# Two transformer blocks on one Trainium2 core: group ends in four steps, filters in the second layer, a reordered beginning

## The chip, the core and the metric

The kernel runs on one core of a Trainium2 chip. PE (TensorE) does the matmuls, PEld is the loading of their stationary operands, DVE (VectorE), ACT (ScalarE) and POOL (GpSimd) do the elementwise work, and SP (SyncE) issues most of the DMAs. The metric is the time of one execution in microseconds (us) on the device; less is better.

## The reference, cut to what matters

The input is x (512 tokens x 1024). Two blocks follow one another, each of two layers. A layer of the first block:

```python
def hybrid_layer(x, ...):
    h = rmsnorm(x, g_pre) @ w_in
    (a_q, a_k, a_v, b_b, b_c, b_x, c_q, c_kv, c_kr, d_q, d_k, d_v, gate) = jnp.split(h, SPLIT_IDX, axis=-1)
    ya = swa_sink_attention(a_q, a_k, a_v, sinks)      # window of 128, 4 heads
    yb = short_gated_conv(b_b, b_c, b_x, conv_w, conv_b)
    yc = mla(c_q, c_kv, c_kr, pos, g_cq, w_uq, g_ckv, w_ukv)
    yd = stick_breaking_attention(d_q, d_k, d_v)
    y = jnp.stack([ya, yb, yc, yd], axis=2)            # four groups of 256 columns
    y = rmsnorm(y, g_grp).reshape(b, s, D_MIX)         # each group by itself
    y = y * jax.nn.silu(gate)
    return x + rmsnorm(y @ w_out, g_post)
```

The second block has, in each layer, a modulation computed from two vectors (`silu(c) @ w_mod`, 1024 x 6144 a layer), attention over tokens and a context, a Fourier mix, a long convolution (Hyena) and a convolutional FFN. The filter of the long convolution depends on weights alone:

```python
def hyena_filter(L, w1, b1, fr1, w2, b2, fr2, w3):
    h = jnp.sin(fr1 * (z @ w1 + b1))                   # z: a fixed embedding of the L positions
    h = jnp.sin(fr2 * (h @ w2 + b2))
    h = h @ w3                                         # 512 columns: forward and backward filter
    two = concatenate([h[:, :256] * decay, 0, (h[:, 256:] * decay)[:0:-1]])
    return two / sum(abs(two), axis=0)
```

Three such filters are needed: for x and the context in the second block's first layer, and for x in its last. So the modulation and the filters need nothing of the first block, and can be computed beside it.

## The kernel before, in words

**Tiles.** Activations lie transposed in SBUF, features on partitions. A large matmul has float32 accuracy through three products of split operands (`mm3`, L560 to L562: high x high, high x low, low x high; L560 to L562 are therefore most of the matmul rows). Every weight tile (128 x 1024 elements, 512 KB) is loaded by SP into one of two `raw` slots and split: ACT copies it to the high part (L528), DVE subtracts for the low part (L529). The same `split` with a factor is L531 and L532.

**The beginning.** `Hybrid.begin` loads the layer's small arrays. SP then loads x in four tiles of 128 tokens (L470, L718). `norm(p)` normalizes two tiles: ACT squares and sums (L576), POOL makes mean and root (L569, L570), DVE scales (L586), PE transposes (L594), ACT and DVE split (L531, L532). `go(p)` multiplies by two kinds of weights that are kept for p = 1: `b_wc` (four tiles, 416 columns a matmul) and `b_wv`. `modulation` begins with a Tanh on ACT (L1306) of an array `cc` that is loaded by ACT's queue, and a DVE operation on it (L1308).

**The weave.** Then `weave` interleaves generators. A generator yields after each step a number, its cost; the generator with the smallest share of its given total goes on next. In a layer of the first block four run together: the attentions (`attention`: MLA's input, stick-breaking, MLA, sliding window), the projections (`dense`: 21 weight tiles `b_wa`, the gates, and last the convolution `conv`), the modulation (`mod_layer`: SP loads `w_mod` into a ring `ws` of four slots, L1336; DVE multiplies and adds, L1340 and L1342), and in layer 0 also `prep`: the sine nets (`filter_nets`, L1192 to L1200), three times `filters` (product L1217, decay L1218, absolute values on ACT L1219, sums L1221 and L1223, a matmul of ones L1227, a reciprocal L1228, output L1234 and L1235) and `fourier_weights` (L1293, of which `bd` is the weight). In layer 1 there is nothing left of `prep`. The written order is then refined by a list scheduler that decides each engine's queue; an engine works its queue in order.

**A group's end.** When an attention or the convolution is done, `finish` ends its group: gate activation, squares on ACT (L1145), products on DVE, one add on POOL (L1149), sums over features as four matmuls with ones (L1153), root on POOL, a scaled identity on DVE (L1161), its split, two matmuls that spread the root over rows (L1171), and the product with the gated values (L1174). The groups are g3 (stick), g2 (MLA), g0 (window), g1 (convolution). The convolution ends last, so g1's end stands at the end of the layer.

**The output projection.** `finish_hybrid` splits the eight feature tiles `z` in the order g3, g2, g0, g1, and `leave` multiplies them with `b_wo`, first for the tokens of two tiles (four PSUM banks, printed f_0 to f_3 by the order), then for the other two.

Of the kernel before, what the change touches and what calls it, by code (L numbers as in the profile page):

```python
# [8 lines left out]
F32 = mybir.dt.float32  # L9
# [261 lines left out]

def drain(gen):
    for _ in gen:
        pass


T = {'a0': 104.76, 'a1': 97.0, 'd0': 108.0, 'd1': 99.36, 'modn': 48, 'm0': 32.659, 'm1': 26.508, 'p0': 93.312, 'sa': 0.859, 'sb': 0.494, 'ml1': 3.5, 'ml2': 2.214, 'sw': 2.584, 'mi': 4.3, 'f1': 2.086, 'f2': 1.452, 'n0a': 181.958, 'n0b': 180.6, 'n1a': 141.12, 'n1b': 72.96, 'rows': 3.84, 'q': 2.496, 'att': 0.7, 'hyp': 1.348, 'spec': 0.544, 'hya': 1.877, 'hyb': 0.828, 'pause': 200, 'cut0': 3, 'cut1': 4, 'cutm': 7, 'foe': 0, 'fse': 0, 'prepn': 99, 'p1': 30.0, 'hye': 1, 'hyf': 1, 'tg': '1', 'ts': '', 'ahead': 1, 'rounds': 3, 'pv': 0}
PAGES = [2048] * 25 + [400]
# [57 lines left out]
def place(log, tries=60):  # L336
# [94 lines left out]
class Net:  # L431
    def __init__(self, tc, ctx, dram, out, places=None):
# [10 lines left out]
        self.wf, self.kd, self.sd, self.L = {}, {}, {}, {}  # L443
        self.setup()
# [79 lines left out]
    def split(self, src, h, l, scale=1.0):  # L524

        nc = self.nc
        if isinstance(scale, float) and scale == 1.0:
            nc.scalar.activation(h, src, AF.Copy)  # L528
            nc.vector.tensor_tensor(l, src, h.bitcast(F32), op=ALU.subtract)  # L529
        else:  # L530
            nc.scalar.activation(h, src, AF.Copy, scale=scale)  # L531
            nc.vector.scalar_tensor_tensor(l, src, scale, h.bitcast(F32), op0=ALU.mult, op1=ALU.subtract)  # L532

# [31 lines left out]
    def rstd(self, ssq, n, dim):  # L565
# [3 lines left out]
        nc.gpsimd.tensor_scalar(r, ssq, 1.0 / dim, EPS, op0=ALU.mult, op1=ALU.add)  # L569
        nc.gpsimd.tensor_tensor(r, r, self.nhalf[:, :n], op=ALU.pow)  # L570
# [8 lines left out]
    def norm(self, xs, hT, at, scale, shift, banks):  # L579
# [3 lines left out]
        for x in xs:  # L583
            y = self.xn(D)
            r = self.rstd(self.square_sum(x, y), 1, D)
            nc.vector.tensor_scalar(y, x, r, None, op0=ALU.mult)  # L586
            ys.append(y)
        h, l = ([a[:, at : at + 256] for a in t] for t in hT)
        for f0 in range(0, KD, 2):
# [5 lines left out]
            for j in range(2):  # L595
                f, src = f0 + j, pt[:, j * 256 : j * 256 + 256]
                if shift is None:
                    self.split(src, h[f], l[f], scale=scale[:, f : f + 1])
# [38 lines left out]
    def leave(self, name, src, order, yT, gain, nxt, cut=4):  # L637
# [4 lines left out]
        self.project(src, order, yT, b[:4], (0, 1), wo, range(KD))  # L642
# [62 lines left out]
    def block1(self):  # L705
# [1556 lines left out]
```

## Time and profile before

| | |
|---|---|
| median of 3 runs | 2264.72 us (2261.48 to 2268.6) |
| profiled execution | 2259.54 us, of which the span is 2257.8 |
| PE busy | 95% of the span |
| DVE busy | 70% |
| ACT busy | 45% |
| POOL busy | 10% |

A span runs from the first to the last instruction of one profiled execution. Times inside it are microseconds from its start. The first 60 us are the beginning, 60.2 to 304.3 is the weave of layer 0, 400.2 to 629.4 that of layer 1.

### The profile page before, as it was taken

The page shows a single profiled execution, that of the slowest core. Times are in us where ns is not written, and L with a number is a line of the kernel's source. Part 1 is how long each engine was busy: PE and PEld are TensorE (multiplying, and loading weights), DVE is VectorE, ACT ScalarE, POOL GpSimd, SP SyncE. Part 2 cuts the span into 40 slices and gives each one's busy share as a digit, 9 for nine tenths or more (in the row PEclk, how much of TensorE's full clock was granted, in tenths as well). Part 3 has the DMA queues.
Part 4 walks back from the last instruction along what each step waited for, and adds up shares of the span by engine and source line. Part 5 has one row for each costly group of instructions (what it writes and reads, how often), then busy time and mean ns, then how long its engine had stood idle before and what let it go on. Part 6 is the DMA issues. An engine that isn't in the chain of part 4 may idle for free.

```text
span 2257.8 us, 30406 instructions
## 1 busy us (share of the span) xinstructions
PE 2147.3 (95%) x11514; PEld 1739.1 (77%) x11514; DVE 1581.9 (70%) x2753; ACT 1018.1 (45%) x1898; POOL 222.2 (10%) x358
## 2 busy tenths in 40 slices
PE   7889989999999898999999999999989999999997
PEld 6656768756777777888888888888668789888886
DVE  5999775668866567587987576766876657456656
ACT  5456434374454355765432232223555655333332
POOL 2022012131021100011000000000320100000001
PEclk9999999999999999999999999999999999999999
DMA  6353242332331123323434123432134022223321
GB/s 210 128 173 123 93 138 81 116 94 84 109 112 47 56 103 113 103 90 103 161 120 156 56 97 119 136 103 92 42 111 143 36 103 85 75 94 112 111 93 57
DMA packets 86354, 235.80 MB, mean 104 GB/s; under 512 B 10576, under 2 KB 12608, under 8 KB 86208
## 3 DMA queue, kind: packets, MB, share of 16 engines
q1 hardware_dynamic: 77424, 219.89, 29.1%
q10 hardware_dynamic: 8784, 13.97, 1.9%
q8 instruction: 90, 1.47, 0.3%
q14 instruction: 56, 0.46, 0.1%
HBM read 225.36 MB, written 8.47 MB: 104 GB/s over the span
## 4 chain that ended last, share of the span: by engine, by line
PE 71%; DVE 8%; ACT 5%; POOL 4%; issue 2%; DMA 2%; DVEq 0%; POOLq 0%; ACTq 0%; SPq 0%
PE f L561 11%; PE f L560 10%; PE f L562 10%; PE b L560 9%; PE b L561 9%; PE b L562 9%; POOL small L570 2%; DVE page L529 2%; PE b L1970 2%; PE b L909 1%; ACT page L528 1%; PE b L908 1%; POOL small L569 1%; PE f L1943 1%; PE f L1031 1%
## 5 line engine op out<-in xcount | busy, mean ns | idle before, releaser
L528 ACT ACTIVATE page<-page 128x1024 fp32r<-128x1024 f32 (+6 forms) x472 | 393.3, 846 | 594.5 <-PE f L561 139.7
L529 DVE TENSOR_TENSOR page<-page,page 128x1024 fp32r<-128x1024 f32 (+6 forms) x472 | 449.3, 964 | 267.6 <-ACT page L528 252.0
L560 PE MATMUL b<-page,page 128*128 128x512 f32 (+3 forms) x1360 | 513.3, 378 | 14.3 <-ACT page L528 5.2
L561 PE MATMUL f<-page,page 128*128 128x512 f32 (+2 forms) x1452 | 523.1, 360 | 3.5 <-DVE page L529 3.5
L560 PE MATMUL f<-page,page 128*128 128x512 f32 (+2 forms) x1456 | 518.6, 361 | 3.4 <-ACT page L605 2.1
L562 PE MATMUL f<-page,page 128*128 128x512 f32 (+2 forms) x1452 | 518.0, 357 | 0.0
L561 PE MATMUL b<-page,page 128*128 128x512 f32 (+3 forms) x1356 | 501.0, 370 | 1.4 <-DVE page L529 1.4
L562 PE MATMUL b<-page,page 128*128 128x512 f32 (+3 forms) x1352 | 498.4, 369 | 3.0 <-DVE page L529 3.0
L560 PEld LDWEIGHTS b<-page,page 128*128 128x128 f32 x1360 | 256.9, 189 | 73.7 <-ACT page L528 13.5
L560 PEld LDWEIGHTS f<-page,page 128*128 128x128 f32 x1456 | 275.1, 190 | 47.4 <-ACT page L528 3.7
L561 PEld LDWEIGHTS f<-page,page 128*128 128x128 f32 x1452 | 274.9, 189 | 44.8 <-DVE page L529 7.9
L562 PEld LDWEIGHTS f<-page,page 128*128 128x128 f32 x1452 | 274.5, 189 | 40.0 <-DVE page L529 1.2
L562 PEld LDWEIGHTS b<-page,page 128*128 128x128 f32 x1352 | 255.4, 189 | 46.9 <-DVE page L529 4.4
L561 PEld LDWEIGHTS b<-page,page 128*128 128x128 f32 x1356 | 256.6, 189 | 43.5 <-issue 4.0
L1342 DVE SCALAR_TENSOR_TENSOR page<-page,page,page 128x512 f32<-128x512 f32 x248 | 179.6, 750 | 5.9 <-DMA page<-w_mod 5.0
L2105 DVE TENSOR_TENSOR page<-b,page 128x512 f32<-128x512 f32 x148 | 100.1, 686 | 65.0 <-PE b L562 64.7
L1429 ACT ACTIVATE page<-f,page 128x512 f32<-128x512 f32 (+1 forms) x128 | 89.3, 698 | 119.7 <-PE f L562 119.5
L569 POOL TENSOR_SCALAR small<-small 128x1 f32<-128x1 f32 (+3 forms) x104 | 43.5, 419 | 820.1 <-DVE small L2116 356.8
L1430 DVE SCALAR_TENSOR_TENSOR page<-f,page,page 128x511 f32<-128x511 f32 (+1 forms) x128 | 83.9, 656 | 40.7 <-ACT page L1429 40.4
L1431 DVE SCALAR_TENSOR_TENSOR page<-f,page,page 128x511 f32<-128x511 f32 (+1 forms) x128 | 84.2, 658 | 3.3
L1948 DVE TENSOR_REDUCE small<-f 128x1 f32<-128x768 f32 (+1 forms) x80 | 66.5, 844 | 27.3 <-PE f L1944 27.0
L570 POOL TENSOR_TENSOR small<-small,nhalf 128x1 f32<-128x1 f32 (+3 forms) x104 | 84.1, 809 | 8.5
(295 smaller groups left out, 2460.4 us busy)
## 6 DMA issues: line engine op xcount, KB each, us to landing
page<-w_mod SPq DMA_DIRECT2D x192, 256.0 KB
page<-b_up SPq DMA_DIRECT2D x88, 512.0 KB
page<-b_dn SPq DMA_DIRECT2D x44, 512.0 KB
page<-b_wa SPq DMA_DIRECT2D x42, 512.0 KB
page<-b_wo SPq DMA_DIRECT2D x40, 512.0 KB
page<-b_wq SPq DMA_DIRECT2D x14, 512.0 KB
page<-b_wkvf SPq DMA_DIRECT2D x12, 512.0 KB
page<-b_wp SPq DMA_DIRECT2D x12, 512.0 KB
```

Of the source, the lines that this page charges most:

```text
L528: nc.scalar.activation(h, src, AF.Copy)
L529: nc.vector.tensor_tensor(l, src, h.bitcast(F32), op=ALU.subtract)
L560: first = nc.tensor.matmul(out, lhsT=ah, rhs=bh, start=start, stop=False, skip_group_check=skip)
L561: nc.tensor.matmul(out, lhsT=ah, rhs=bl, start=False, stop=False, skip_group_check=skip)
L562: nc.tensor.matmul(out, lhsT=al, rhs=bh, start=False, stop=stop, skip_group_check=skip)
L570: nc.gpsimd.tensor_tensor(r, r, self.nhalf[:, :n], op=ALU.pow)
L1342: nc.vector.scalar_tensor_tensor(acc[:, s], w, c, acc[:, s], op0=ALU.mult, op1=ALU.add)
L1429: nc.scalar.activation(o, ps, AF.Identity, scale=taps[:, 1:2], bias=taps[:, 3:4])
L1430: nc.vector.scalar_tensor_tensor(o[:, 1:], ps[:, : n - 1], taps[:, 0:1], o[:, 1:], op0=ALU.mult, op1=ALU.add)
L1431: nc.vector.scalar_tensor_tensor(o[:, : n - 1], ps[:, 1:], taps[:, 2:3], o[:, : n - 1], op0=ALU.mult, op1=ALU.add)
L1948: nc.vector.tensor_reduce(mx, s, axis=AX.X, op=ALU.max, negate=True)
L2105: nc.vector.tensor_tensor(o, ps, o, op=ALU.add)
```

## The change

Instructions are the same in number but for 18 matmuls of zeros. Line numbers after the change are larger: L577 to L579 are `mm3` (560 to 562 before), L1215 the sums of a group (L1153), L1237 its rows (L1171), L1285 the filters' product (L1217), L1406 the loads of `w_mod` (L1336).

**The beginning.** The loads of the last two x tiles wait in a list and are issued after the second and third tile of `b_wc`'s first half. 18 matmuls of zeros are put ahead of the first norm. Forced orders (`after`) put each first root on POOL ahead of the next mean, the Tanh of `modulation` behind the first norm's splits, its DVE operation and the low part of a weight tile behind the first norm's scaling. `mod_layer` of layer 0 uses a ring of three slots that is there anyway (`wd`).

**The filters.** Layer 0's weave takes from `prep` only the two steps of the sine nets; all the rest goes into layer 1's weave.

**The group ends.** `finish` is cut into four steps: squares and add; sums; scale; rows. For g3 and g2 the last three are alternated with the steps of the next attention (`beside`). g1's end is kept as `tail`: one step of it is taken ahead of each of the output projection's weight tiles 1 to 5, and the rest, with the split of g1's own features, ahead of tile 6.

```diff
+def beside(gen, other):
+    while True:
+        try:
+            yield next(gen)
+        except StopIteration as e:
+            yield from other
+            return e.value
+        yield next(other, 0.0)
...
-def place(log, tries=60):
+def place(log, tries=600):
...
-        for t in range(2, NT):
-            nc.sync.dma_start(self.x[:, t, :], self.d["x"][t])
-        for p in range(2):
-            h.norm(p, self.pt)
-            h.go(p)
+        self.later = [lambda t=t: nc.sync.dma_start(self.x[:, t, :], self.d["x"][t]) for t in range(2, NT)]
+        for _ in range(WARM):
+            nc.tensor.matmul(b[7], lhsT=self.zb[:, :P], rhs=self.zb, start=True, stop=True)
+        h.norm(0, self.pt)
+        begun = [self.scaled], [self.halved]
+        self.starting, self.roots, self.ahead = False, [], [self.scaled]
+        h.go(0)
+        h.norm(1, self.pt)
+        h.go(1)
         MARK("mod")
-        mod = self.modulation()
+        mod = self.modulation(*begun)
...
-            self.weave_hybrid(l, [(self.some(mod, 48 if l == 0 else 96), 50.0)] + ([(self.some(prep, T["prepn"]), T["p0"])] if l == 0 else [(prep, T["p1"])]))
+            self.weave_hybrid(l, [(self.some(mod, 48 if l == 0 else 96), 50.0)] + ([(self.some(prep, 2), 93.0)] if l == 0 else [(prep, 20.0)]))
...
-        for f in order:
-            self.split(self.z[f], zT[0][f], zT[1][f])
-            self.free(self.z[f])
-        self.leave(f"b1.{l}", self.d["b1_wo"][l], order, zT, gpost, nxt, T[f"cut{l}"])
+        def before(n):
+            tail, ys = self.tail
+            if n == 6:
+                drain(tail)
+                self.free(ys, self.fin, self.finr, self.vec)
+                ready(order[6:])
+            elif n:
+                next(tail, None)
+        ready(order[:6])
+        self.leave(f"b1.{l}", self.d["b1_wo"][l], order, zT, gpost, nxt, T[f"cut{l}"], before)
...
-        yield from self.stick(l, self.sbqk)
-        yield from self.mla_att(l)
+        ys = yield from self.stick(l, self.sbqk)
+        yield from self.wait(3)
+        end = self.finish(l, 3, ys)
+        yield next(end)
+        ys = yield from beside(self.mla_att(l), end)
...
         self.gate_act(g)
-        self.group_squares(g, ys)
-        yield T["f1"]
-        self.group_scale(g)
-        yield T["f2"]
+        y2 = self.group_squares(g, ys)
+        yield T["f1"] / 2
+        self.group_sums(g, y2)
+        yield T["f1"] / 2
+        parts = self.group_scale(g)
+        yield T["f2"] / 2
+        self.group_rows(g, parts)
+        yield T["f2"] / 2
...
-        yield from self.finish(l, 1, ys)
-        self.free(ys)
+        self.tail = self.finish(l, 1, ys), ys
...
-        ws, accs = self.ring(512, 4), self.ring(1024, 3)
+        ws, accs = self.ring(512, 4) if l else self.wd, self.ring(1024, 3)
```

SP's queue at the start, before. `x` are the tiles of the input, `b_wc` and `b_wv` the weights of `go`, `b_uq` and `b_ukv` those of MLA's input:

```order
L470 DMA x<-x 128x1024 x2
L718 DMA x<-x 128x1024 x2
L538 DMA page_0_85<-b_wc 128x832 x2
L847 DMA page_23_96<-b_uq 128x768
L1336 DMA page_23_96<-w_mod 128x512
L1336 DMA page_15_93<-w_mod 128x512
L538 DMA page_0_85<-b_wc 128x832 x2
L538 DMA page_0_85<-b_wv 128x768 x4
```

The same queue after the change:

```order
L483 DMA x<-x 128x1024 x2
L555 DMA page_0_85<-b_wc 128x832 x2
L742 DMA x<-x 128x1024 x2
L899 DMA page_70_530<-b_uq 128x768
L555 DMA page_0_85<-b_wc 128x832 x2
L900 DMA page_42_104<-b_ukv 128x512
L1406 DMA page_12_92<-w_mod 128x512 x3
L555 DMA page_0_85<-b_wv 128x768 x4
```

The first two weight tiles now stand ahead of the last two x tiles, and the next two ahead of the first loads of `w_mod`.

PE's queue at the end of layer 0, before: b_63 takes the convolution's last products, b_65 the sums of g1, f_0 to f_3 the output projection.

```order
L560 MATMUL b_63<-page_29_101,page_2_86 128x512
L561 MATMUL b_63<-page_39_103,page_2_86 128x512
L562 MATMUL b_63<-page_29_101,page_4_87 128x512
L1153 MATMUL b_65<-ones,page_90_787 128x128 x4
L560 MATMUL f_0_70<-page_164_2247,page_25_100 128x512
L560 MATMUL f_1_71<-page_164_2247,page_25_100 128x512
L560 MATMUL f_2_72<-page_164_2247,page_25_100 128x512
L560 MATMUL f_3_73<-page_164_2247,page_25_100 128x512
```

After the change, at the same place (b_66 takes the sums):

```order
L577 MATMUL f_2_72<-page_33_102,page_131_2103 128x512
L578 MATMUL f_2_72<-page_33_102,page_131_2103 128x512
L579 MATMUL f_2_72<-page_33_102,page_128_2101 128x512
L577 MATMUL f_3_73<-page_33_102,page_131_2103 128x512
L578 MATMUL f_3_73<-page_33_102,page_131_2103 128x512
L579 MATMUL f_3_73<-page_33_102,page_128_2101 128x512
L1215 MATMUL b_66<-ones,page_84_601 128x128 x4
L577 MATMUL f_0_70<-page_31_100,page_131_2103 128x512
```

Before, the sums stand right behind the convolution's last product. Now 24 matmuls of the output projection (two weight tiles) stand between them, and another 24 between the sums and the rows (L1237).

PE's queue in the stick-breaking attention of layer 0, before: L989 begins that attention's sums with zeros, L945 and L969 are its own products, L1217 the filters' first.

```order
L989 MATMUL f_2_72<-zb 128x512
L945 MATMUL f_0_70<-page_77_544 128x128
L945 MATMUL f_1_71<-page_77_544 128x128
L989 LDWEIGHTS zb
L989 MATMUL f_3_73<-zb 128x512
L1217 MATMUL b_63<-page_66_502,page_71_514 128x512
L1217 MATMUL b_64<-page_66_502,page_71_514 128x512
L1217 MATMUL b_63<-page_66_502,page_71_514 128x512
L969 MATMUL f_0_70<-page_98_845,page_25_100 128x128 x2
```

After the change the filters' first product stands in layer 1, beside MLA's input (L911, L920):

```order
L579 MATMUL b_64<-page_33_102,page_4_87 128x512
L1285 MATMUL b_63<-page_23_95,page_15_93 128x512
L911 MATMUL f_0_70<-page_197_2754,page_178_2322 128x384 x2
L920 MATMUL f_1_71<-page_180_2323,page_178_2322 128x512
L1285 MATMUL b_64<-page_23_95,page_15_93 128x512
L929 MATMUL b_65<-ident,page_8_91 96x128 x4
```

In layer 0 the place of these products is taken by 35 matmuls of the projections, which now stand between L989 and the stick-breaking attention's next product.

## Rows read from the trace of the kernel before

**Rows 1.** The page: busy time of each engine, share of the span, number of instructions.

```profile
PE 2147.3 (95%) x11514; PEld 1739.1 (77%) x11514; DVE 1581.9 (70%) x2753; ACT 1018.1 (45%) x1898; POOL 222.2 (10%) x358
```

**Rows 2.** Windows: stretch, length, busy PE PEld DVE ACT POOL, granted clock, DMA, GB/s.

```profile
0.00:60.00 60.00, 44.95 (x236) 40.30 (x237) 31.98 (x79) 29.05 (x64) 12.92 (x34) 1.00 0.61 199
60.20:304.30 244.10, 225.21 (x1014) 155.17 (x1012) 222.12 (x481) 123.02 (x262) 38.84 (x63) 0.97 0.40 129
400.20:629.40 229.20, 217.37 (x1050) 153.68 (x1048) 171.67 (x398) 111.18 (x249) 36.76 (x66) 1.00 0.32 102
100.00:165.00 65.00, 52.96 (x194) 32.12 (x194) 63.32 (x111) 36.74 (x71) 15.09 (x28) 0.89 0.45 155
450.00:515.00 65.00, 61.44 (x255) 38.21 (x254) 45.30 (x79) 46.37 (x101) 25.94 (x53) 1.00 0.31 97
309.00:312.40 3.40, 3.03 (x11) 2.84 (x12) 0.92 (x2) 1.06 (x1) 0.99 (x2) 0.50 0.54 157
```

**Rows 3.** Timeline of the start: start, length, engine, line, what ended its wait.

```profile
0.85 0.52 POOL L482 MEMSET zb<- 128x512 bf16 x1
7.53 1.07 POOL L570 TENSOR_TENSOR small<-small,nhalf 128x1 f32<-128x1 f32 x2
9.80 0.18 DVE L1308 SCALAR_TENSOR_TENSOR small<-small 128x16 f32<-128x16 f32 x1 [8.53 <-ACT small L1306]
10.10 1.42 DVE L586 TENSOR_SCALAR page<-x,small 128x1024 f32<-128x1024 f32 x2
10.91 2.20 PE L594 MATMUL b<-ident,page 128*128 128x128 f32 x8 [10.91 <-DVE page L586]
13.04 1.06 PE L560 MATMUL f<-page,page 128*128 128x416 f32 x2
16.69 1.09 PE L594 MATMUL b<-ident,page 128*128 128x128 f32 x8 [0.20 <-DVE page L532]
18.20 0.35 PE L561 MATMUL f<-page,page 128*128 128x416 f32 x1
18.39 0.35 PE L562 MATMUL f<-page,page 128*128 128x416 f32 x1
```

**Rows 4.** PE's waits: line waiting, line waited for, total us, times, longest.

```profile
PE b L1153 <- POOL page L1149: 9.4, 8, 4.7
PE b L1171 <- ACT page L531: 3.5, 5, 0.9
```

**Rows 5.** Costliest groups, window 60 to 165: busy, mean ns | idle before, releaser.

```profile
L1217 PE MATMUL b<-page,page 128*128 128x512 f32 x20 | 12.9, 759 | 5.7 <-ACT page L1197 5.2 <-DVE page L1218 0.4
L1234 DVE TENSOR_TENSOR page<-page 128x256 f32<-128x256 f32 x20 | 8.0, 441 | 0.0
L1293 PE MATMUL b<-page,page 128*128 128x256 f32 x16 | 5.5, 508 | 3.0 <-DMA page<-bd 3.0
L1223 DVE TENSOR_TENSOR page<-page 128x256 f32<-128x256 f32 x3 | 1.6, 530 | 0.0
```

**Rows 6.** Timeline of the end of layer 0, by engine.

```profile
304.28 0.40 PE L562 MATMUL b<-page,page 128*128 128x512 f32 x1
309.37 2.07 PE L1153 MATMUL b<-ones,page 128*128 128x128 f32 x8 [4.69 <-POOL page L1149]
311.10 1.78 PE L560 MATMUL f<-page,page 128*128 128x512 f32 x4
...
306.60 2.72 POOL L1149 TENSOR_TENSOR page<-page,page 128x512 f32<-128x512 f32 x1 [16.93 <-ACT page L1145]
...
306.98 1.22 DVE L529 TENSOR_TENSOR page<-page,page 128x1024 fp32r<-128x1024 f32 x1
```

**Rows 7.** The add L1149 over the whole run: least, median, longest ns.

```profile
L1149 POOL TENSOR_TENSOR page<-page,page x7: 1281/1291/2717, 200.8 to 627.6; 128x512 f32<-128x512 f32 x7
```

**Rows 8.** SP's waits: total us, times, longest.

```profile
SPq L538 <- DVE page L529: 946.7, 204, 37.2
SPq L1336 <- DVE page L1342: 215.8, 141, 9.3
```

More of the change, by code (lines that the diff above doesn't have):

```diff
@@ L443, in __init__ @@
         self.wf, self.kd, self.sd, self.L = {}, {}, {}, {}
+        self.roots, self.starting, self.later, self.ahead = [], True, [], []
         self.setup()
@@ L528, in split @@
             nc.scalar.activation(h, src, AF.Copy)
-            nc.vector.tensor_tensor(l, src, h.bitcast(F32), op=ALU.subtract)
+            low = nc.vector.tensor_tensor(l, src, h.bitcast(F32), op=ALU.subtract)
+            if self.ahead:
+                self.after(low, self.ahead)
+                self.ahead = []
         else:
-            nc.scalar.activation(h, src, AF.Copy, scale=scale)
+            first = nc.scalar.activation(h, src, AF.Copy, scale=scale)
             nc.vector.scalar_tensor_tensor(l, src, scale, h.bitcast(F32), op0=ALU.mult, op1=ALU.subtract)
+            return first
     def wload(self, src, n, keep=False):
@@ L568, in rstd @@
         r = self.small(n)
-        nc.gpsimd.tensor_scalar(r, ssq, 1.0 / dim, EPS, op0=ALU.mult, op1=ALU.add)
-        nc.gpsimd.tensor_tensor(r, r, self.nhalf[:, :n], op=ALU.pow)
+        mean = nc.gpsimd.tensor_scalar(r, ssq, 1.0 / dim, EPS, op0=ALU.mult, op1=ALU.add)
+        if self.roots:
+            self.after(mean, self.roots)
+        root = nc.gpsimd.tensor_tensor(r, r, self.nhalf[:, :n], op=ALU.pow)
+        if self.starting:
+            self.roots = [root]
         return r
@@ L635, in residual, with leave @@
         nc.vector.scalar_tensor_tensor(x, tmp, r, x, op0=ALU.mult, op1=ALU.add)
-    def leave(self, name, src, order, yT, gain, nxt, cut=4):
+    def leave(self, name, src, order, yT, gain, nxt, cut=4, before=None):
         b, x = self.b, self.x
@@ L641, in leave @@
         MARK(f"{name} out")
-        self.project(src, order, yT, b[:4], (0, 1), wo, range(KD))
+        for n in range(KD):
+            if before:
+                before(n)
+            self.project(src, order, yT, b[:4], (0, 1), wo, (n,))
         for t in range(2):
@@ L763, in finish_hybrid, with ready @@
         order = [2 * g + j for g in (3, 2, 0, 1) for j in range(2)]
-        for f in order:
-            self.split(self.z[f], zT[0][f], zT[1][f])
-            self.free(self.z[f])
-        self.leave(f"b1.{l}", self.d["b1_wo"][l], order, zT, gpost, nxt, T[f"cut{l}"])
+        def ready(fs):
+            for f in fs:
+                self.split(self.z[f], zT[0][f], zT[1][f])
+                self.free(self.z[f])
+        def before(n):
[6 more added lines that the diff above has]
+                next(tail, None)
+            MARK(f"b1.{l} out")
+        ready(order[:6])
+        self.leave(f"b1.{l}", self.d["b1_wo"][l], order, zT, gpost, nxt, T[f"cut{l}"], before)
     def mtile(self, l, u):
@@ L833, in attention @@
             yield from self.wait("sins")
-        yield from self.stick(l, self.sbqk)
-        yield from self.mla_att(l)
+        ys = yield from self.stick(l, self.sbqk)
[3 more added lines that the diff above has]
+        ys = yield from beside(self.mla_att(l), end)
         yield from self.wait("a")
-        yield from self.swa(l, self.swqk)
+        yield from self.wait(2)
+        end = self.finish(l, 2, ys)
+        yield next(end)
+        yield from beside(self.swa(l, self.swqk), end)
     def wait(self, what):
@@ L1000, in stick @@
         self.free(after, parts, later, qk)
-        yield from self.finish(l, 3, ys)
+        return ys
     def finish(self, l, g, ys):
@@ L1052, in mla_att @@
         self.free(self.qT, self.kT, self.vc, prs, pTs)
-        yield from self.finish(l, 2, ys)
+        return ys
     def softmax(self, p, s, mask, scale):
@@ L1617, in half @@
                 ws[kk] = net.wload(src[kk], 2 * n, keep=True)
+                if kk and net.later:
+                    net.later.pop(0)()
             for i in range(2):
```

38 lines of the change are left out of this document (27 added, 11 removed).

## The prediction

> **What bounds the kernel now.** I read the page's busy shares first: PE works 95% of the span and no other engine over 70% [rows 1]. The limit is PE, so a change can only give back microseconds in which PE waits or runs slowly, or create such ones. What the change moves is work of DVE, ACT and POOL and some short PE work; only 18 matmuls are added. So I asked, stage by stage, how much PE loses where the change acts, and whether the place the work goes to has room.
>
> The windows answer per stage [rows 2]. In the beginning PE is busy 44.95 of 60 us, idle 15.05. In the weave of layer 0 it is busy 225.2 of 244.1 us (92.3%), idle 18.9, at a mean granted clock of 0.97; in that of layer 1, 217.4 of 229.2 (94.8%), idle 11.8, at 1.00. The reader is to see DVE in the same lines: 222.1 of 244.1 us (91%) in layer 0, 171.7 of 229.2 (75%) in layer 1. The layer with filters runs with a nearly full DVE. The list of PE's waits then has the group ends [rows 4]: 9.4 us for the sums behind POOL's add, of which one wait is 4.7, and 3.5 for the rows behind a split. The timeline places that 4.69 at the end of layer 0 [rows 6]; two of this size make the 9.4, one for each layer, so g3, g2 and g0 have next to nothing to gain.
>
> **The beginning: -8.** PE's first transposes wait for DVE's scaling until 10.91. The two roots it needs ended by 7.53 + 1.07 = 8.60 (the row merges both; the first by half of that, near 8.1). It stood in DVE's queue behind L1308, which waited until 9.80 for the Tanh, and began at 10.10 [rows 3]. The forced order takes this away. The pair takes 1.42 and ended at 11.52. With the first scaling from 8.1 and the second from 8.60, each 0.71 to 0.75 long, it ends at 9.35: -2.2; with both only from 8.60, at 10.0: -1.5. I take the first, since the roots are now forced apart. Then pace: eight transposes take 2.20 us at first and 1.09 at 16.69, so -1.1; the ten 416-column matmuls from 13.04 to 16.49 start about 0.53 apart in their first pair and 0.19 apart at 18.20, so ten at the later pace are about 1.5 shorter [rows 3]. The windows show a granted clock of 1.00 for the whole 60 us [rows 2], so the slower pace is seen in the durations only, and that zeros ahead cure it is my assumption. The zeros cost nothing if they end before the first transpose: their operand is ready at 0.85 + 0.52 = 1.37 [rows 3], four 512-column matmuls at the low pace take 1.78, 0.45 each [rows 6], so 18 end by 9.5 at the latest, some 0.1 late. Last, the weights: of the 15.05 idle, 10.91 is ahead of the first matmul and 4.1 behind it. The first two weight tiles now pass two x tiles on SP and the next two pass `w_mod`; I take 3 of the 4.1, between 0 and all. The sum is -2.2 - 1.1 - 1.5 - 3 = -7.8; bounds -4.1 and -8.9. The x tiles that come later are needed only for p = 1, after some 90 matmuls, which covers them; without this cover each would cost its load.
>
> **The group ends: -11.** The waits are 9.4 + 3.5 = 12.9 [rows 4]. After the wait at the end of layer 0 PE runs 3.4 us at a granted clock of 0.50 [rows 2], which is the lower level, 1.2 GHz, and it had stood still for 4.69 before. Half of 3 us is lost; if the wait goes, so does this: 1.5, counted once because only this stretch has a row. In all 14.4. The chain itself stays (convolution, square, add, sums) but 24 matmuls now stand in it. At the low level a product of 512 columns takes 0.45 (four in 1.78), so 0.22 at the high one, and 24 take 5.3 us, against 4.69 of waiting [rows 6]. The next 24 stand in front of the rows, whose longest wait was 0.9 [rows 4]. This cover is there if the output projection's first weight tiles are split by then. Before, such a tile's subtraction runs at 306.98 for 1.22 [rows 6]; if it comes no earlier now, PE waits for it instead, up to 308.2 - 304.7 (the end of the last product, 304.28 + 0.40) = 3.5 in each layer, and only 14.4 - 7 = 7.4 is gained; the 1.5 may not come either, so the bounds are -6 and -14.4. I take a lateness of about 1 us in each layer and the rest of the clock's 1.5 as uncertain: -11. The steps of g3 and g2 that now run beside MLA and the window attention stand in PE's in-order queue ahead of those attentions' transposes; what they may cost is a rival.
>
> The Trainium skill bears on the add, in "SBUF — State Buffer", section "Who interferes with whom": VectorE and GpSimd share a pair of ports that is locked for a whole instruction, and a VectorE operation with two SBUF inputs blocks a GpSimd operation that reads SBUF. The trace agrees as far as it goes: the add at 306.60 took 2.72 us while DVE's subtraction of two SBUF tiles (1.22 us) lay in it [rows 6], where the median of these adds is 1.29 [rows 7].
>
> **The filters: -7.** Their direct waits in layer 0 are 5.2 (first product, for the sine net on ACT) and 3.0 (the load of `bd`) [rows 5]. In the stretch from 100 to 165 us PE idles 12.0 of 65 us at a granted clock of 0.89; in the same part of layer 1's weave, 450 to 515, it idles 3.6 at 1.00 [rows 2]. The difference is 8.5 us of idling and, of the clock, about 0.11 x 65 = 7 us of which PE worked on long matmuls perhaps two thirds of the time, 4.5. So layer 0 gives -13. Layer 1 takes work: the filters' DVE operations are six groups, from 8.0 us (L1234) to 1.6 (L1223), 33.6 in all (the others 6.7, 6.7, 5.4, 5.2) [rows 5], and DVE there would stand at 171.7 + 33.6 = 205 of about 242 us, 85%, between the two cases seen. PE idles 5.2% at 75% of DVE and 7.7% at 91%; at 85%, by the line between, 6.8%, or +1.6% of 240, some 4 us; two more for waits of their own: +6. Net -7.
>
> The same by shares: the filters' large PE groups are 12.9 + 5.5 = 18.4 us [rows 5]. Layer 0 without them at layer 1's share takes (225.2 - 18.4) / 0.948 = 218.1, -26.0. Layer 1 with them takes 235.8 / 0.948 = 248.6, +19.4, at its own share: net -6.6; at layer 0's share, 235.8 / 0.923 = 255.6, +26.4: net +0.4. The bounds are -13 (nothing given back) and +4 (all waits return, and DVE's 4 on top). Against a return of all: the sine nets stay in layer 0, so the 5.2 has no cause left, and a yield now stands between the load of `bd` and its use.
>
> **The sum** is made against the profiled 2259.5 us (span 2257.8 + 1.7): -8 - 11 - 7 = -26, so 2233.5. The median of the runs is 5.2 above that execution; for the median I forecast 2264.7 - 26 = **2239**.
>
> **The rivals.**
> - *Layer 1 gives nothing back.* For it: DVE's 75% there [rows 2]. Then the filters are worth -13: 2264.7 - 8 - 11 - 13 = 2233, and with all terms at their good ends (-8.9 - 14.4 - 13) 2228.
> - *The move of the filters is worth nothing.* For it: DVE at 85%, and the share of layer 0 as it is now. 2264.7 - 19 = 2246 with 0, 2250 with +4.
> - *The group ends' wait only moves,* to the first weight tiles of the output projection, or to the attentions in whose queue the sums now stand: -6 instead of -11, 2244. Both of these last together, with the beginning at -4.1: 2264.7 - 6 - 4.1 + 4 = 2259, no change.
> - *The adds take longer.* They run now beside attentions and an output projection full of DVE subtractions. Each at 2.72 instead of 1.29 costs 1.4 if uncovered, in two layers 2.8: 2242. This is what the rule of the Trainium skill in "SBUF — State Buffer", "Who interferes with whom", would make of it. Against it: the one add in front of which PE waited at the end of layer 0 was already a long one.
> - *The zeros do nothing for the pace.* Then 2.6 of the beginning stays: 2242.
> - *Slower: the ring of three.* SP's queue is in order. It waits 141 times, 215.8 us, for DVE to free a slot of the `w_mod` ring [rows 8], and the loads of `b_wa`, 21 a layer, stand behind. With three slots instead of four each such wait starts earlier, and the weights may reach PE late. It decides from where the 42 loads come late to PE by more than 26 / 42 = 0.62 us each (no gain left), and is slower by over 0.3% at 33 / 42 = 0.79 each: 2272 or more. Against it: the weight loads themselves wait for their slot, 946.7 us in 204 times, 4.6 each [rows 8], so they are asked for ahead of need.
>
> **How the numbers follow.** Three runs of before differ by 7 us, so about 0.3% (6.8 us) is what a measurement can tell from no change. Chances: the forecast 0.38, own range 2232 to 2246; nothing given back 0.14; the filters' move worth nothing 0.16 (0.02 of it together with the weak ends, as no change); the wait only moves 0.10 (0.01 likewise); longer adds 0.04; zeros without effect 0.04; the ring 0.14, of which 0.08 slower and 0.06 no change. So slower 0.08, same 0.06 + 0.03 = 0.09, faster 0.83. The range goes from 2220 (the good ends' 2228 less a spread of runs) to 2261 (the 2259 of the weak cases with a little of the same), with some 0.12 left out above and 0.06 below.
>
> **What would show it.** The first 416-column matmul at about 10.5 instead of 13.04, and started 0.19 after its neighbour; the weave of layer 0 beginning near 52 and lasting about 219, with no long wait of the filters' products and a granted clock of 1.00; that of layer 1 lasting about 248, DVE near 85%; PE's wait for the sums near 1 instead of 9.4 and no stretch at 0.50 after a layer's end. The prediction is wrong if layer 1 grows as much as layer 0 shrinks, if a wait for split weights takes the place of the sums' wait, or if SP's waits for the `w_mod` ring grow and PE's for weights with them.

## The result

| | median us | runs | range |
|---|---|---|---|
| before | 2266.66 | 4 | 2261.48 to 2270.59 |
| changed | 2243.06 | 4 | 2237.60 to 2245.31 |

The ratio is 0.9897, 95% interval 0.9885 to 0.9910: faster by 1.03%, 23.3 us of 2264.7, where 26 were forecast. The sum came out, but by luck: of its three large terms two were off by half or more, in opposite directions (e1 and e3 below).

The page's busy times after the change:

```profile
PE 2147.1 (96%) x11532; PEld 1741.3 (78%) x11532; DVE 1580.8 (70%) x2753; ACT 1013.5 (45%) x1898; POOL 221.7 (10%) x358
```

PE's busy time is the same to 0.2 us, the zeros included [rows 1]. The span is 14.7 us shorter in the two profiled executions, and all but 0.2 of that is idle time of PE. The runs differ by more, 23.3, because this execution (2244.83 us) was among the slower of its four, while the profiled one of before (2259.54) was faster than all four of before. So the stages below add up to 14.7 and not to 23.3.

Windows of the changed kernel (columns as in [rows 2]): the beginning, the weave of layer 0 from its first to its last projection matmul, and that of layer 1, which had 229.2 us, to its last group's sums. The fourth line is the kernel before, layer 0, from its own first projection matmul:

```profile
0.00:60.00 60.00, 53.26 (x269) 45.19 (x269) 40.88 (x95) 30.41 (x70) 13.26 (x34) 0.94 0.66 216
60.00:274.90 214.90, 207.25 (x960) 145.41 (x959) 180.29 (x405) 115.34 (x248) 37.95 (x63) 0.99 0.33 100
367.10:612.40 245.30, 233.24 (x1104) 162.16 (x1102) 206.32 (x458) 120.02 (x266) 37.93 (x66) 1.00 0.42 131
62.50:304.30 241.80, 224.38 (x1010) 154.96 (x1010) 219.82 (x476) 121.88 (x259) 38.84 (x63) 0.97 0.40 129
```

Layer 0 takes 214.9 instead of 241.8 us, with PE busy 96.4% instead of 92.8. (The 244.1 of [rows 2] begin 2.3 us ahead of the first projection matmul.) Layer 1 takes 245.3 instead of 229.2, and there PE is busy 95.1%, as much as the 94.8 before, though DVE has gone from 75% to 84%. The weaves together give 26.9 - 16.1 = 10.8. The first projection matmul of layer 0 starts at 59.97 instead of 62.53, so the beginning gives 2.6. From the sums of layer 1 to the end, which is its output projection and the second block, nothing is won (1630.7 us, 1628.4 before).

The list of PE's waits, changed kernel (line waiting, line waited for, us, times, longest); the last line is the first one's counterpart in the kernel before:

```profile
PE f L578 <- DVE page L542: 8.3, 9, 2.3
...
PE b L577 <- ACT page L541: 6.1, 5, 2.1
PE f L577 <- ACT page L541: 5.1, 5, 2.2
...
PE b L1215 <- POOL page L1207: 2.5, 3, 1.5
...
PE b L1237 <- ACT page L547: 1.1, 2, 0.7
...
PE f L561 <- DVE page L529: 3.5, 4, 2.1
```

The sums' wait fell from 9.4 to 2.5 and the rows' from 3.5 to 1.1 [rows 4]. What grew is PE's wait for split weights in the `f` rows, among them the output projection's (8.3 us for the subtraction, 3.5 before; it is in the second block too).

The timeline of the end of layer 0, changed kernel, in those rows that waited or belong to the group's end:

```profile
280.42 1.05 PE L1215 MATMUL b<-ones,page 128*128 128x128 f32 x8
...
282.46 0.50 PE L577 MATMUL f<-page,page 128*128 128x512 f32 x1 [0.99 <-ACT page L541]
...
283.72 0.50 PE L578 MATMUL f<-page,page 128*128 128x512 f32 x1 [0.76 <-DVE page L542]
...
289.07 0.82 PE L1237 MATMUL b<-page,ones 128*128 128x512 f32 x2
...
291.19 0.50 PE L578 MATMUL f<-page,page 128*128 128x512 f32 x1 [1.07 <-DVE page L542]
```

The sums start without a wait and run at full pace (eight in 1.05 us, 2.07 before [rows 6]). Three waits of 0.76 to 1.07 us for split weights follow: the lateness that the prediction allowed for, 1 us a layer, is 2.8 here.

### The profile page after: what moved, and what is told of

The parts are those of the page before. It is cut to its first block, busy times and chain, and to the rows that moved or that the text cites. A ratio compares the mean times of both kernels' runs of the same rounds, so it can differ in the third digit from the quotient of the medians.

```text
span 2243.1 us, 30425 instructions
## 1 busy us (share of the span) xinstructions
PE 2147.1 (96%) x11532; PEld 1741.3 (78%) x11532; DVE 1580.8 (70%) x2753; ACT 1013.5 (45%) x1898; POOL 221.7 (10%) x358
## 4 chain that ended last, share of the span: by engine, by line
PE 69%; DVE 13%; DMA 6%; ACT 5%; POOL 4%; issue 3%; SPq 0%; DVEq 0%; ACTq 0%; POOLq 0%
PE f L578 9%; PE f L579 9%; PE f L577 9%; PE b L577 9%; PE b L579 9%; PE b L578 9%; DVE page L542 4%; ACT page L541 3%; POOL small L589 2%; PE b L2044 2%; DMA page<-b_wo 2%; PE b L961 1%; DVE page L1412 1%; PE b L960 1%; PE f L2017 1%
## 5 line engine op out<-in xcount | busy, mean ns | idle before, releaser
L541 ACT ACTIVATE page<-page 128x1024 fp32r<-128x1024 f32 (+7 forms) x472 | 392.5, 846 | 596.9 <-PE f L578 138.7
L542 DVE TENSOR_TENSOR page<-page,page 128x1024 fp32r<-128x1024 f32 (+7 forms) x472 | 448.3, 964 | 269.7 <-ACT page L541 255.6
L577 PE MATMUL f<-page,page 128*128 128x512 f32 (+2 forms) x1456 | 518.6, 360 | 8.9 <-ACT page L541 5.1
L577 PE MATMUL b<-page,page 128*128 128x512 f32 (+3 forms) x1356 | 510.3, 377 | 11.4 <-ACT page L541 6.1
L579 PE MATMUL f<-page,page 128*128 128x512 f32 (+2 forms) x1444 | 516.6, 358 | 0.8 <-DVE page L542 0.8
L579 PE MATMUL b<-page,page 128*128 128x512 f32 (+3 forms) x1340 | 496.2, 371 | 4.7 <-DVE page L542 4.6
L577 PEld LDWEIGHTS f<-page,page 128*128 128x128 f32 x1456 | 276.5, 190 | 50.0 <-ACT page L541 7.9
L577 PEld LDWEIGHTS b<-page,page 128*128 128x128 f32 x1356 | 256.4, 189 | 67.1 <-issue 11.1
L579 PEld LDWEIGHTS f<-page,page 128*128 128x128 f32 x1444 | 274.6, 190 | 38.9 <-DVE page L542 2.7
L579 PEld LDWEIGHTS b<-page,page 128*128 128x128 f32 x1340 | 253.8, 189 | 48.8 <-DVE page L542 8.1
L1412 DVE SCALAR_TENSOR_TENSOR page<-page,page 128x512 f32<-128x512 f32 x183 | 132.8, 752 | 3.5 <-DMA page<-w_mod 2.8
```

Of the source, the lines that this page charges most:

```text
L542: low = nc.vector.tensor_tensor(l, src, h.bitcast(F32), op=ALU.subtract)
L577: first = nc.tensor.matmul(out, lhsT=ah, rhs=bh, start=start, stop=False, skip_group_check=skip)
L579: nc.tensor.matmul(out, lhsT=al, rhs=bh, start=False, stop=stop, skip_group_check=skip)
L1412: nc.vector.scalar_tensor_tensor(acc[:, s], w, c, acc[:, s], op0=ALU.mult, op1=ALU.add)
```

## The experiments

Each kernel was timed in five rounds against the kernel before. The us behind a ratio are the ratio's difference from 1 times 2264.7. An experiment changes more than its name says. The traces of e4, e5, e6 and e9 show the engines' queues in another order than before, in the second block too, and stages that an edit does not touch move by some microseconds; e5, further down, shows by how much.

| run | ratio | 95% interval | us |
|---|---|---|---|
| the change | 0.9897 | 0.9885 to 0.9910 | -23.3 |
| e1 beginning alone | 0.9985 | 0.9977 to 0.9994 | -3.4 |
| e2 group ends alone | 0.9965 | 0.9953 to 0.9977 | -7.9 |
| e3 filters moved, ring of three | 0.9932 | 0.9919 to 0.9945 | -15.4 |
| e4 ring of three alone | 1.0081 | 1.0068 to 1.0093 | +18.3 |
| e5 other places alone | 1.0005 | 0.9996 to 1.0014 | +1.1 |
| e6 ring of three, other places | 1.0065 | 1.0052 to 1.0079 | +14.7 |
| e7 changed, no zeros | 0.9892 | 0.9878 to 0.9905 | -24.5 |
| e8 changed, splits first | 0.9880 | 0.9867 to 0.9894 | -27.2 |
| e9 own ring of three alone | 1.0123 | 1.0107 to 1.0138 | +27.9 |
| e10 changed, fourth slot | 0.9954 | 0.9941 to 0.9966 | -10.4 |
| e11 splits first, fourth slot | 0.9951 | 0.9938 to 0.9963 | -11.1 |
| e12 changed, ends as before | 0.9945 | 0.9932 to 0.9957 | -12.5 |

### The parts alone: e1 to e3

The theory is the prediction's sum; the rival is that its terms were mis-sized and met by chance. Each of e1 to e3 has one part of the diff that is shown above. e1 (with the ring of four):

> The beginning alone: loads, zeros and forced orders, with the ring of four. By the terms of the prediction it gives -8 us. By the trace after, in which the first projection matmul of layer 0's weave starts at 59.97 us instead of 62.53, it gives -2.6: DVE waits for the load of the positions (1.09 us) ahead of the first low splits, and that wait takes the place of the one removed.

It gave -3.4: the rival's size, not -8. e2:

> The group ends in four steps alone. By the terms of the prediction -11 us (between -6 and -14.4), PE's wait for the sums near 1 instead of 9.4 us. If the wait only moves to the first weight tiles of the output projection, -6 or less, and waits for L529 or L528 of that size appear ahead of the f matmuls at the ends of both layers.

It gave -7.9, between the two. The sign of the first expectation held: PE's wait for the sums is 0.9 us in e2 (two of 0.5 at most). Ahead of the output projection at the ends of the layers there are waits for split weights of 0.3 to 1.1 us, as in the changed kernel. e3 has, besides the two lines on `prep`, the costs of the generators' steps that go with them, and the ring of three:

> The filters in the second layer alone, with the ring of three and the 600 tries of the page placement, without which it finds no room. By the terms of the prediction -7 us: layer 0 about -26, layer 1 about +19. If DVE in layer 1 holds PE up as in layer 0, 0. If layer 1 gives nothing back, -13.

It gave -15.4, twice the forecast and a little beyond the rival in which layer 1 gives nothing back. Its windows, the weaves of layers 0 and 1 to the sums of the last group, and below them layer 0 of the kernel before:

```profile
62.70:280.90 218.20, 210.05 (x978) 146.74 (x978) 189.94 (x420) 115.42 (x250) 39.83 (x65) 1.00 0.34 106
366.50:611.20 244.70, 230.61 (x1083) 160.32 (x1082) 203.06 (x454) 117.97 (x260) 37.79 (x68) 0.99 0.40 126
62.50:310.40 247.90, 225.78 (x1015) 155.99 (x1016) 223.72 (x481) 124.86 (x262) 41.55 (x64) 0.97 0.39 128
```

Layer 0 needs 218.2 us up to the same point where the kernel before needed 247.9, -29.7 with a granted clock of 1.00. Layer 1 grows by 15.5, of which 13.2 is PE work that moved in and 2.3 is idle time of PE; that idle time is what the rival means by giving back. The three parts add up to -26.7, the change as a whole gives -23.3: additive within the intervals.

### The ring of three: e4, e5, e6 and e9

The prediction gave the smaller ring a cost of nothing, with a slower rival.

```diff
-        ws, accs = self.ring(512, 4), self.ring(1024, 3)
+        ws, accs = self.ring(512, 4) if l else self.wd, self.ring(1024, 3)
```

> The ring of three for the modulation's weights and the 600 tries alone, nothing else changed. By the prediction's sum 0 (within 2 us); by the slower rival, weights late by 0.6 to 0.8 us in 42 loads, +26 to +33, and PE's waits for L529 and L528 grow by as much.

The ring costs 18.3 us in the kernel before. Any change of what is allocated also changes where in SBUF all tiles lie, and with that which operation waits for which to leave a place, so this was tried by itself and with the ring:

```diff
-T = {..., 'pause': 200, ...}
+T = {..., 'pause': 100, ...}
```

> The kernel before with its tiles placed otherwise in SBUF (a parameter of the placement, 100 for 200); no instruction added or removed. If the +16.5 us of the ring of three come from the ring, this stays within 3 us of before. If they come from the tiles' new places, which decide what waits for what, this moves by some microseconds as well, and in the second block too.

> The ring of three alone, with the same other placement as in the run on places. If the ring costs, this stays 13 to 20 us above that run. If the +16.5 was the placement's, the difference to that run is within 5 us.

Other places alone change nothing in the sum (+1.1), and with the ring the kernel is 13.6 above that. So the loss goes with the ring, at two placements. Whether with the number of slots or with their being shared:

```diff
-        ws, accs = self.ring(512, 4), self.ring(1024, 3)
+        ws, accs = self.ring(512, 4 if l else 3), self.ring(1024, 3)
```

> The kernel before with three slots of its own for the modulation's weights in layer 0, not shared with other tiles. If the +15 us of the shared ring of three come from one slot less, this stands 10 to 16 us above before, with DVE waiting for w_mod loads in layer 0. If they come from sharing (the slots are also used by the filters' last step and by the second block), it is within 4 us of before.

Three slots of its own cost 27.9, so the loss does not need the sharing. DVE's waits in layer 0 from 60 to 320 us, e4 and then e9 (columns as in the list of PE's waits):

```profile
DVE page L1354 <- DMA page<-w_mod: 7.4, 5, 3.5
```

```profile
DVE page L1342 <- DMA page<-w_mod: 5.4, 5, 2.0
```

In the kernel before there is no wait for `w_mod` in that stretch. So DVE, 91% busy there, now also stands still for its own loads. The slower rival's path, weights that come late to PE through SP's queue, shows only a little: PE's waits of L969 for the split weights in that weave are 2.3 us before, 2.7 in e4, 5.6 in e9, 7.6 in e6. SP's waits for the ring did not grow as it said (215.8 us before [rows 8], 194.4 in e4, 197.0 in e9). What these waits of DVE and PE add is 8 to 11 us, if all of DVE's are counted, and not 15 to 28.

The windows show that much of the rest does not lie beside the ring at all. A stretch from layer 1's sums to an output projection in the second block, where no `w_mod` is loaded any more, in the kernel before, in e4 and in e5:

```profile
629.90:807.70 177.80, 166.58 (x802) 134.94 (x801) 108.10 (x218) 77.48 (x156) 28.78 (x46) 0.97 0.22 74
635.10:822.50 187.40, 172.04 (x818) 139.74 (x818) 108.16 (x218) 78.89 (x157) 26.80 (x44) 0.95 0.21 71
627.60:811.60 184.00, 166.53 (x793) 133.21 (x792) 107.10 (x218) 77.72 (x156) 27.29 (x45) 0.96 0.21 70
```

e4 loses 9.6 us here, and of the 23.1 by which its span is longer than that of before, 18.4 lie behind layer 1's sums (in e9 20.6 of 33.8). Other places alone (e5) move this stretch by 6.2, and two others by 3.0 and 3.6 the other way. With the second placement it is otherwise: e6's span is 14.4 longer than e5's, and all of it lies ahead of layer 1's sums. So the ring's loss is measured as a whole, but it has no fixed place; that a missing slot makes it, and not the new order and places that come with the edit, is not shown.

### The ring in the changed kernel: e10 and e11

```diff
-        ws, accs = self.ring(512, 4) if l else self.wd, self.ring(1024, 3)
+        ws, accs = self.ring(512, 4) if l else Ring(self.wd.slots + [self.new(512)]), self.ring(1024, 3)
         for r in range(6):
+            if r == 3 and not l:
+                self.free(ws.slots[3])
+                ws = self.wd
```

> The changed kernel with a fourth slot for the modulation's weights during layer 0's weave. If the ring of three still costs there, 4 to 15 us faster than the changed kernel. If the cost hangs on a full DVE in layer 0, as it is with the filters there (91%) and no longer without them (84%), within 3 us of the changed kernel.

Neither: with the fourth slot it is 12.9 us slower than the changed kernel. Windows of e10, the weave of layer 0 to the sums, up to layer 1's first weights, layer 1 to its sums, and the beginning of the second block; below them the same four of the changed kernel:

```profile
61.40:271.00 209.60, 202.00 (x966) 144.78 (x964) 185.42 (x414) 114.32 (x247) 36.08 (x62) 1.00 0.36 109
271.00:326.40 55.40, 47.84 (x215) 37.57 (x214) 37.63 (x54) 21.80 (x42) 8.85 (x16) 1.00 0.33 105
326.40:619.70 293.30, 275.14 (x1289) 199.23 (x1290) 226.94 (x490) 135.45 (x302) 48.02 (x88) 0.97 0.41 127
619.70:1011.80 392.10, 364.23 (x2251) 302.66 (x2250) 249.59 (x458) 213.36 (x445) 48.27 (x64) 0.97 0.26 85
```

```profile
60.00:281.00 221.00, 213.34 (x990) 150.49 (x989) 186.17 (x412) 115.97 (x249) 39.42 (x64) 0.99 0.34 104
281.00:329.00 48.00, 42.60 (x192) 33.32 (x190) 34.45 (x50) 22.24 (x41) 6.41 (x12) 1.00 0.42 128
329.00:612.90 283.90, 269.30 (x1292) 196.69 (x1293) 224.82 (x488) 135.71 (x302) 49.65 (x90) 0.99 0.41 127
612.90:1001.80 388.90, 363.27 (x2252) 300.42 (x2251) 250.31 (x462) 212.04 (x446) 47.29 (x64) 0.98 0.27 87
```

The weave of layer 0 is 11.4 us shorter and the output projection 7.4 longer, but most of that exchange is the boundary: 24 matmuls fewer stand ahead of e10's sums (966 against 990). Over both windows e10 is 4.0 us shorter, and PE's idle time in them is 15.2 us against 13.1. So the fourth slot removes no waiting of PE there; what is shorter is PE's busy time at the same number of matmuls (249.8 us against 255.9), in part by pace (a granted clock of 1.00 against 0.99 up to the sums). The boundary of layer 1 is shifted too: four of e10's eight sums stand at 613.07, the other four 20 output products later. To the first of them layer 1 takes 286.7 us against 283.4, and another 9.4 us are lost behind them. The ring drops back to three where layer 1's weave begins, so this run does not tell what four slots throughout would do; that was not tried. Like the loss of the ring, this one lies where the slot is not in use, and no cause is shown for it.

> The reordered splits of the run before and the fourth slot together. The gains add if they are independent: the changed kernel -5 for the splits and what the fourth slot gives by itself.

It did not add: -11.1, as e10 alone.

### The beginning: e7 and e8

Rows of the changed kernel's beginning (timeline as in [rows 3]), PE and then, between its two products, what DVE did:

```profile
7.83 0.44 PE L615 MATMUL b<-ident,page 128*128 128x128 f32 x2 [0.46 <-DVE page L607]
...
9.60 2.19 DVE L542 TENSOR_TENSOR page<-page,page 128x832 fp32r<-128x832 f32 x2 [0.36 <-ACT page L541]
...
11.29 0.46 PE L577 MATMUL f<-page,page 128*128 128x416 f32 x1 [1.11 <-ACT page L547]
...
11.97 0.42 PE L578 MATMUL f<-page,page 128*128 128x416 f32 x1
...
12.88 0.17 DVE L694 CAST small<-pos 128x4 f32<-128x4 int32 x1 [1.09 <-DMA pos<-pos]
...
13.46 0.87 DVE L548 SCALAR_TENSOR_TENSOR page<-b,page,page 128x256 fp32r<-128x256 f32 x2
...
13.99 1.06 PE L579 MATMUL f<-page 128*128 128x416 f32 x2 [1.60 <-DVE page L548]
...
15.20 0.55 PE L578 MATMUL f<-page,page 128*128 128x416 f32 x1
```

The first two transposes come at 7.83, 3 us earlier, the other six at 9.30, and at full pace. Then two weight subtractions (2.19 us) and an operation on the positions, which waits 1.09 for its load, stand in DVE's queue ahead of the low part of x, and PE waits until 13.99. Windows of the time ahead of that wait, of the wait, of what follows, and the one from 10 to 20:

```profile
7.80:12.00 4.20, 2.02 (x12) 1.52 (x12) 2.81 (x3) 2.63 (x4) 0.57 (x2) 1.00 1.05 388
12.00:12.40 0.40, 0.38 (x2) 0.00 (x0) 0.00 (x0) 0.00 (x0) 0.00 (x0) 0.63 1.04 378
12.40:14.00 1.60, 0.01 (x1) 0.01 (x1) 1.05 (x5) 0.03 (x1) 0.00 (x0) 0.50 1.05 427
14.00:18.60 4.60, 4.60 (x16) 4.38 (x17) 3.47 (x12) 2.82 (x6) 0.00 (x0) 0.50 1.03 393
10.00:20.00 10.00, 7.28 (x29) 6.44 (x28) 7.57 (x20) 5.83 (x11) 0.00 (x0) 0.66 1.04 395
```

The granted clock is 0.50, 1.2 GHz, for the 4.6 us from 14.0 on. But it was not the wait of 1.6 us that took it down: the clock falls between 12.0 and 12.4, while PE still works. What lies ahead of the fall is a stretch in which PE was busy 2.02 of 4.20 us, with waits of 1.03 and 1.11. The pace that the zeros had given is taken back here. Without them:

```diff
-WARM = 18
+WARM = 0
```

> The changed kernel without the 18 matmuls of zeros. By the prediction's term +2.6 us (transposes and first ten matmuls at half the pace). By the trace after, where PE stands still for 1.6 us at 12.4 and then runs 4.6 us at a granted clock of 0.50, most of what the zeros give is lost again: 0 to +1.

0.9892 against 0.9897: the zeros are worth nothing that these runs can measure. e8 moves the second weight tile's splits and the operation on the positions out of the way:

```diff
+        nc.scalar.dma_start(self.pos, self.d["pos"])      # ahead of h.begin()
...
-        nc.vector.tensor_copy(pf, pos)
+        self.after(nc.vector.tensor_copy(pf, pos), self.lows[:2])
...
-        self.starting, self.roots, self.ahead = False, [], [self.scaled]
+        self.starting, self.roots, self.ahead = False, [], [([self.scaled], []), (self.lows[:2], self.highs[:2])]
```

(`highs` and `lows` collect the two halves of the first splits of x; the second weight tile's two halves are put behind them.)

> The changed kernel with the positions loaded at the very start, DVE's operation on them and both splits of the second weight tile put behind the first splits of the normalized x. If the beginning fell short because those stood ahead of the splits, the third product of the first tile starts near 11 instead of 13.99 us, there is no stretch at 0.50 at 14, and the first projection matmul comes 3 to 5 us earlier than 59.97; the whole is faster by about that, unless another placement of tiles hides it. If the weights' loads are the limit, the waits only move to the later weight tiles and the gain is under 1.

Its first rows on PE, and its windows from 10 to 20, 20 to 30, and the whole beginning:

```profile
10.63 0.46 PE L582 MATMUL f<-page,page 128*128 128x416 f32 x1 [0.38 <-ACT page L548]
...
11.30 0.35 PE L584 MATMUL f<-page 128*128 128x416 f32 x1
...
13.10 0.46 PE L582 MATMUL f<-page,page 128*128 128x416 f32 x1 [1.07 <-ACT page L548]
...
22.68 0.65 PE L582 MATMUL f<-page,page 128*128 128x416 f32 x2 [1.12 <-ACT page L541]
```

```profile
10.00:20.00 10.00, 7.58 (x40) 6.04 (x39) 6.00 (x15) 6.09 (x13) 0.04 (x1) 1.00 1.02 383
20.00:30.00 10.00, 8.18 (x36) 7.30 (x35) 6.96 (x24) 5.25 (x15) 4.13 (x10) 0.83 0.67 197
0.00:60.00 60.00, 53.16 (x261) 43.91 (x261) 38.51 (x89) 29.70 (x67) 13.91 (x34) 0.97 0.64 212
```

The third product of the first tile starts at 11.30 as wanted, and there is no half clock at 14. But PE waits later instead, up to 22.68 for weight tiles, the low clock moves to the stretch from 20 to 30, and the first projection matmul comes at 59.74, 0.2 earlier. For the beginning the second expectation held. DMA is full (share 1.02, 383 GB/s) from 10 to 20 us in this run, in the changed kernel (1.04, 395) and in the kernel before (1.02, 374): this suggests that the transfers set the beginning's end, but it is argued and not shown. The whole is -27.2, the lowest of these ratios; its interval and the changed kernel's overlap, and the gain is not where it was looked for (layer 1's first weights at 326.1 instead of 329.0).

### The group ends in place: e12

> The changed kernel with the group ends as before. By the terms of the prediction +11 us; by the run of the group ends alone +8; if the filters' move took part of the same waits, +2 to +5, PE's waits for the sums at the ends of the layers being shorter than 4.7 us already.

-12.5 against -23.3: the kernel with the steps is faster by 10.8 by the ratios and 6.7 by the medians (2249.75 against 2243.06), so by no less than alone. It is not where the 4.69 stood. With the filters gone PE waits only 0.63 us for the sums at the end of layer 0 in e3, without any steps. At the end of layer 1, e12, with the windows from there of e12 and of the changed kernel:

```profile
611.57 1.17 PE L1180 MATMUL b<-ones,page 128*128 128x128 f32 x8 [1.88 <-POOL page L1176]
...
611.50:616.00 4.50, 3.92 (x15) 3.13 (x16) 3.06 (x6) 1.28 (x2) 1.23 (x3) 0.62 0.92 318
612.30:617.00 4.70, 4.16 (x21) 3.26 (x21) 2.58 (x5) 1.65 (x2) 1.22 (x3) 1.00 0.29 108
```

There the wait is 1.88, and 1.48 in the changed kernel. From these sums (612.1) to the same output products of the second block e12 needs 181.7 us (to 793.8), the changed kernel 174.0 (612.9 to 786.9), the kernel before 177.8. The difference lies behind the layer's end. A part of it is pace: the granted clock there is 0.62 in e12 and 1.00 in the changed kernel. Whether the rest is the steps' is not shown, since other places alone move this same stretch by 6.2 us (184.0 in e5).

## Why the prediction was right, and where not

**The sum** came out by luck. Measured alone, the beginning and the group ends gave 4.6 and 3.1 us less than forecast and the filters 8.4 more; these misses cancel. The ring of three, put at nothing, is in the last of them.

**The bound** was read rightly: PE's busy time stayed the same to 0.2 us, the zeros included, and its idle time fell by 14.5.

**The beginning: -8 forecast, -3.4 measured alone.** The step that failed is "I take 3 of the 4.1" with "-1.1" and "-1.5" for the pace. The scaling came free of the Tanh as said (the pair ends at 9.24, forecast 9.35). But the next thing in DVE's queue was late: the load of the positions, which ACT's queue issued at 6.43 us before and at 9.85 now, behind the splits of the weights. The prediction asked what was behind L1308 and not what would then be ahead of L548. And the pace: zeros ahead did give the high level (six transposes in 0.88 us, without zeros 1.54), but the granted clock fell again at 12 us, after a stretch in which PE was busy half the time. e7 prices the zeros at nothing.

**The group ends: -11 forecast, -7.9 alone, 7 to 11 in place by e12.** Alone it is within its bounds; in place the steps' share is not shown, as said at e12. One step was wrong: "two of this size make the 9.4, one for each layer". The wait at the end of layer 1 before was 1.54 us; the 9.4 were 4.69 and seven short ones:

```profile
629.36 1.65 PE L1153 MATMUL b<-ones,page 128*128 128x128 f32 x8 [1.54 <-POOL page L1149]
```

The cover worked: 2.5 us of the sums' wait are left, and waits of about 1 us for split weights took their place, 2.8 at the end of layer 0 where 1 a layer was allowed for.

**The filters: -7 forecast, -15.4 with the ring of three.** Layer 0 was right by the shares: -26.0 forecast, -26.9 in the changed kernel from the first projection matmul to the last, and 0.97 of clock back to 0.99. Layer 1 was not: +19.4 forecast, +16.1 measured. The failed step is "by the line between, 6.8%", with which the direct sum made +6 for layer 1: DVE went to 84%, as forecast (85%), and PE did not idle more for it (12.1 us, 11.8 before; 4.9% against 5.2). So in the changed kernel the rival was right in which layer 1 gives nothing back, and e3 lies near its -13. What the ring of three takes or gives within e3 is open. Two layers at 75% and 91% don't make a line; of the 9.8 us by which PE idles less in layer 0, particular waits are 8.2, the sine net (5.2) and `bd` (3.0), and these are gone: the filters' product has no wait in layer 1. The row of the costliest groups, changed kernel, 367 to 613 us:

```profile
L1285 PE MATMUL b<-page,page 128*128 128x512 f32 x20 | 10.5, 608 | 0.0
```

**The ring: 0 forecast, +15 to +28 measured in the kernel before.** The slower rival, with 0.14 of the chance, had the direction. Its mechanism is seen only in a small part: weights later by 0.4 to 5.3 us, and 5 to 7 of DVE's own waits, which it had not named; SP's waits for the ring did not grow. Its price by itself is mostly below the 26 to 33 that it named, and where the loss comes from stays open. It did not decide, because the move of the filters is worth 33.7 us on top of a ring of three (e3 against e4). In the changed kernel DVE's wait for `w_mod` in layer 0 is 1.1 us once, and the stretch behind layer 1's sums is 2.3 us longer than before, not 18.

**The adds** do not take longer than the one of before. Their row over the whole run, changed kernel (least, median, longest ns), and those of the product L1204 on DVE, which reads one tile from PSUM (`f`) or both from SBUF:

```profile
L1207 POOL TENSOR_TENSOR page<-page x8: 1266/1284/1782, 175.6 to 610.5; 128x512 f32<-128x512 f32 x8
...
L1204 DVE SCALAR_TENSOR_TENSOR page<-f,page,page x12: 737/744/751, 171.2 to 575.6; 128x512 f32<-128x512 f32 x12
L1204 DVE SCALAR_TENSOR_TENSOR page<-page,page x2: 1751/1764/1778, 276.9 to 611.1; 128x512 f32<-128x512 f32 x2
```

The longest add was 2717 before [rows 7]; now the two at the layers' ends take 1472 and 1782. But the rule of the Trainium skill in "SBUF — State Buffer", "Who interferes with whom", was not without effect. The trace agrees with it on the other side: the two products of L1204 that took 1.75 and 1.78 us instead of 0.74 are those that read two SBUF tiles and began while an add was running (at 276.64 and 610.53). Those that read PSUM took at most 0.75, beside an add as without one. What the 2 us of DVE cost the whole is not shown.

## What to carry to other kernels

Where work is moved off a path, read the queue of the engine that was freed: the next instruction in it may wait for something that was hidden until then, here a load of 2 KB. The stage with the full engine lost here mostly by a few waits that can be named, and not by a share; price a move by such waits at the new place and not by a line through two layers. And a buffer given up to make room is a change of its own: the ring of three, alone, cost more than the beginning and the group ends together brought, and most of that lay in other stages in two kernels (e4, e9) and none of it in a third (e6). Look at the stages that an edit does not touch before a difference of a few microseconds is put down to it.

## What was not expected of the hardware and the program

The granted clock fell to 0.50 (1.2 GHz) at 12 us though PE had not stood still for longer than 1.11 us since its first transposes; it had been busy 2.02 of 4.20 us. Before the change PE's first 4.6 us of work ran at about half the pace while the granted clock of that window stood at 1.00 [rows 2, 3]: at a program's start this column doesn't show the pace. A product of two SBUF tiles on DVE took 1.75 to 1.78 us instead of 0.74 when it began during POOL's add. New places in SBUF for the tiles moved the whole by 0.05% (e5) but one stretch by 6.2 us, and a ring of three moved the whole by 0.6% to 1.2%.
